# Other orders of the same work in a hybrid decoder block: z blocks ahead for one SSM unit, gate tiles loaded elsewhere, three FFN blocks side by side, last residual pairs by halves

## The chip, the core and the metric

The kernel runs on one core of a Trainium2 chip. The metric is the time of one execution in microseconds (us) of device time. Five engines work side by side, each in the order of its own queue: TensorE (PE: matrix products, with PEld for its weight loads), VectorE (DVE), ScalarE (ACT), GpSimd (POOL) and SyncE (SP, which here issues DMAs). A wait for another engine's result stops everything that stands behind it in the same queue.

## The reference

One decoder block over 256 positions of width 2048, in fp32. Two token mixers read the same normed input and are merged by sigmoid gates; a SwiGLU FFN follows.

```python
h = modulate(rms_norm(x, w), shift, scale)          # adaLN from c
ssm_z, ssm_xbc, ssm_dt, gdn_qkv, gdn_z, gdn_beta, gdn_a, gate_ssm, gate_gdn = split(h @ w_in)
y_ssm = mamba2_ssd_mixer(ssm_z, ssm_xbc, ...) @ w_ssm_proj     # conv, chunked scan, norm, 8 groups
y_gdn = gated_deltanet_mixer(gdn_qkv, gdn_z, ...) @ w_gdn_proj # conv, triangular solve, scan, 32 heads
m = sigmoid(gate_ssm) * y_ssm + sigmoid(gate_gdn) * y_gdn
x = x + gate * (m @ w_o)
x = x + gate2 * ffn(modulate(rms_norm(x), ...))     # silu(a) * b, then w_dn
out = rms_norm(x, w)
```

## The kernel before, in words

All weights come in blocks of 128 x 1024 fp32 (512 KB). For every block `load_next` issues the DMA into `raw` on SP's queue, lets ACT copy it to `hi` (L146) and DVE take `lo = raw - hi` (L148), so that a product is made of three: hi*hi, hi*lo and lo*hi. A block is one item of a queue. It costs TensorE 24 matmuls of 128 x 256 (L221 to L223, `lin_items`; L245 to L247, `quad_items`) or, for the z blocks, 12 of 128 x 512 (L268 to L270, `z_items`).

`pump()` is the clock of the program text. Each call loads blocks until four are ready, issues the matmuls of the oldest one, takes at most a few of the waiting posts (what follows a finished bank: convolution, gate, residual) and then one step of the running mixer, which is a Python generator: a `yield n` lets about n*R blocks pass before the next step. R is `RG[hu]` for the Gated DeltaNet (GDN) units `gdn_mix`, hu = 0 to 7, and `R_S` for the SSM units `ssm_mix`, g = 0 to 7. A block with `need` or `late_need` may be issued only when so many mixers are done; while it stands first in the queue, only mixer steps are issued, with no matmuls of weights between them.

While a unit is mixed, the blocks of the next unit are the cover: `g_in` and `s_in` append twelve to sixteen blocks for q, k, v or x, B, C and eight z blocks, and `proj_items` appends eight blocks that multiply the unit before by its output matrix (w_gp or w_sp) and add it to `accg` (L592). In the first SSM unit the eight w_gp blocks also gate the sum: `gate_g_post` (L984) reads a tile `ggt` that `gg_load` (L977) fetches from DRAM into one of two buffers.

The mixer steps that matter below, by the names of their tiles: at the head of a GDN unit `squares` and `ssq` (sums of squares of q and k), `N`/`T` and `seg` (decay exponents: `seg_rhs` makes the inputs on ACT, `seg_exp` two matmuls and an exp), `kq`; later `Tm` and `tv`; at its end `var`, `o` and `ot` (norm and transposition of the output, with a reciprocal root of 12 small POOL operations between). In an SSM unit `xt`, `cb`, `rh`/`rl` and `seg`, `yb`, `yo`, `yt`.

After the last unit come the merge, w_o, the second norm (`rf`, then 16 tiles `h2h`/`h2l`), w_gu, w_dn and the final norm. `res_post` adds a finished bank to the residual `accs` in two halves (L1204) and squares it (L1206); `ps_sq` sums the squares over partitions. At the FFN's entry `quad_items` cuts K into four quarters: an item of w_gu needs four h2 tiles only, and pairs of banks take their first quarters one after the other.

Of the kernel before, what the change touches and what calls it, by code (L numbers as in the profile page):

```python
# [19 lines left out]
P = 128  # L20
# [16 lines left out]

RG = [1.0] * 7 + [0.95]
R_M = 1.2
Q3 = [0, 8, 1, 9, 2, 10, 3, 11, 4, 12, 5, 13, 6, 14, 7, 15]  # L40
Y_SUB = [7] + [9] * 7
R_S = 1.6
# [32 lines left out]
def block_kernel(ctx: ExitStack, tc: tile.TileContext, xT, cvec, vec, dskip, consts,  # L75
# [132 lines left out]

    def lin_items(blocks, xh, xl, nk, done, need=0, sync=False, late_need=0):
        hold = {}  # L210
# [14 lines left out]
        for bi, src in enumerate(blocks):  # L225
            last = bi == len(blocks) - 1
            post = [lambda f=f: f(hold["ps"]) for f in done] if last else []
            add_item(src, mk(bi), post, late_need if last and late_need else need, sync and bi == 0)

    def quad_items(src, n, xh, xl, done, sync=False):  # L230
        bank_of = {}

        def mk(q, j):
            def mm(hi, lo):
                ah, al = xh(), xl()
                if q == 0:
                    bank_of[j] = plin.tile([P, 2, S], F32, tag="lin", name="ps_lin") if j < 3 else \
                        bank("ps_lin", (P, 2, S))
                ps = bank_of[j]
                for t in range(2):  # L240
                    for k in range(4):
                        kt = 4 * q + k
# [11 lines left out]

    def z_items(blocks, unit, extra=None):
        pss = {}
# [23 lines left out]
        for b in range(8):  # L280
            ex = extra[len(extra) * b // 8:len(extra) * (b + 1) // 8] if extra else []
            add_item(blocks[b], mk(b), ([lambda: done(0), lambda: done(1)] if b == 7 else []) + ex)

# [335 lines left out]

    def s_in(g, need=0, extra=None):  # L620
        unit = {}
        for pr in range(3):
            i = 6 * g + 2 * pr
            lin_items([w_s[g, 4 * pr + b] for b in range(4)], hh, hl, KT,
                      conv_posts(lambda ps: ps, VC_S + 4 * i, VCB_S + i, in_tile(unit, pr, 6)),
                      late_need=need if pr == 0 else 0)
        z_items(w_sz[g], unit, extra)
        return unit
# [87 lines left out]
    def gdn_mix(hu, units):  # L716
        unit = units[hu]
        nxt = units[hu + 1] if hu + 1 < NHU else None
        if hu == 0:
# [4 lines left out]
            seg_in, seg_out, squares, ssq, kq, scales, n_tile, store = gdn_head(hu, unit)  # L724
            squares()
            seg_in(0)
            yield 1
            ssq()
            seg_out(0)
            yield 1  # L730
            seg_in(1)
            kq()
            yield 1
            seg_out(1)
# [73 lines left out]
        for c in range(2):  # L808
            V.tensor_tensor(Tm[c].rearrange("p h (b j) -> p h b j", j=16),
                            Tp[:, 4 * c:4 * c + 4, :].unsqueeze(2).broadcast_to([P, 4, 8, 16]),  # L810
                            mid(bmask.rearrange("p (b j) -> p b j", j=16), 4), MUL)
        yield 1 if hu == 0 else 2
        for c in range(2):
# [175 lines left out]
    def ssm_mix(g, unit):  # L989
# [115 lines left out]
    for g in range(NG):  # L1105
        gens.append((ssm_mix(g, unit[NHU + g]), mark + DS, R_S if g < 7 else 1.0))
        if g + 1 < NG:
            gg = [lambda: None] * 6 + [lambda: gg_load(0), lambda: None]
            unit.append(s_in(g + 1, G0 + NHU + g, gg if g == 0 else None))
        else:  # L1110
# [88 lines left out]
    def res_post(j, gate, pool):  # L1199
        def f(ps):  # L1200
            x2 = pools["accs"]
            for t in range(2):
                i = 2 * j + t
                V.scalar_tensor_tensor(x2[:, i, :], ps[:, t, :], gate[:, i:i + 1], x2[:, i, :], MUL, ADD)  # L1204
            sq = pool.tile([P, 2, S], F32, tag="th" if j else "cacc", name="sq", bufs=1 if j or pool is not gl_ else NCA)
            A.activation(sq, x2[:, 2 * j:2 * j + 2, :], AF.Square)  # L1206
            if j == 0:
                sqa["a"] = sq
            elif j < 7:
                G.tensor_tensor(sqa["a"], sqa["a"], sq, ADD)  # L1210
            else:
                sqa["b"] = sq
        return [f]

    quad_items(w_o, 3, lambda: pools["m"][0], lambda: pools["m"][1], lambda j: res_post(j, ada[:, 32:48], gl_), sync=True)
    for j in range(3, 8):
        lin_items([w_o[j, b] for b in range(4)], lambda: pools["m"][0], lambda: pools["m"][1], KT,
                  res_post(j, ada[:, 32:48], gl_))
    n_wo = st_["added"]
# [32 lines left out]
    with tc.tile_pool(name="ff", bufs=1) as ff:  # L1252
# [7 lines left out]
        for t in range(KT + 1):  # L1260
            if t in (5, 9, 13):
                for _ in range(6):
# [12 lines left out]
        for j in range(8):  # L1275
            lin_items([w_dn[j, b] for b in range(11)], fh, fl, FT, res_post(j, gf, ff))
        ada_fin(80, 96)
# [116 lines left out]
```

## Time and profile before

| what | value |
|---|---|
| timed executions | median 2765.83 us (2764.89 to 2770.86, 3 runs) |
| profiled execution | 2744.2 us |
| its span, first to last instruction | 2742.4 us |
| mean granted TensorE clock | 0.988 |
| busy in the span | TensorE 97%, DVE 69%, ACT 50%, POOL 11% |

The profiled execution is 21.6 us shorter than the timed median; what is worked out from the trace is a difference and is carried over to the median as it stands.

### The profile page before, as it was taken

How to read it: one execution, taken by the hardware profiler on the slowest of the kernel's cores; microseconds unless marked ns; L12 is line 12 of the kernel's file. 1: busy time of each engine (PE TensorE's matmuls, PEld its weight loads, DVE VectorE, ACT ScalarE, POOL GpSimd, SP SyncE). 2: the span in 40 equal slices, each digit the busy share in tenths (PEclk: the TensorE clock that was granted, in tenths of full speed). 3: DMA queues.
4: the chain of work that ended last, by engine and by line, in shares of the span. 5: the costliest groups of instructions: out<-in, count | busy, mean ns of one | idle time of the engine just before them, and what ended most of it. 6: DMA issues, size and time to landing. Idle time of an engine off the chain costs nothing.

```text
span 2742.4 us, 51781 instructions
## 1 busy us (share of the span) xinstructions
PE 2665.7 (97%) x20930; PEld 2547.5 (93%) x20930; DVE 1884.0 (69%) x2794; ACT 1371.5 (50%) x2250; POOL 306.7 (11%) x684
## 2 busy tenths in 40 slices
PE   6999999999999999989999999999999999999998
PEld 5889899999999999988899989999989999999997
DVE  7787767769687786857767667768666666655444
ACT  3325554655546455544666656554444444444442
POOL 0000312303123131210000000002100000000000
PEclk8999999999999999999999999999999999999999
DMA  8886657566575665735545445447756666655553
GB/s 334 299 325 231 208 173 253 182 208 229 168 248 175 227 213 173 253 131 179 190 156 177 167 163 176 162 153 268 241 178 216 228 224 225 228 199 194 192 193 131
DMA packets 183283, 566.90 MB, mean 207 GB/s; under 512 B 34753, under 2 KB 43777, under 8 KB 183041
## 3 DMA queue, kind: packets, MB, share of 16 engines
q1 hardware_dynamic: 154306, 552.56, 59.0%
q10 hardware_dynamic: 28736, 11.01, 1.5%
q8 instruction: 164, 2.69, 0.4%
q14 instruction: 77, 0.63, 0.1%
HBM read 552.49 MB, written 11.01 MB: 205 GB/s over the span
## 4 chain that ended last, share of the span: by engine, by line
PE 64%; issue 21%; DVE 6%; DMA 4%; POOL 3%; ACT 2%; SPq 0%; ACTq 0%; DVEq 0%; POOLq 0%
PE ps_lin L221 14%; PE ps_lin L223 14%; PE ps_lin L222 14%; PE ps_z L268 2%; PE ps_z L270 2%; PE ps_z L269 2%; DMA araw<-in_w_ada 2%; DVE lo L148 2%; PE ps_lin L246 1%; PE tw L831 1%; PE td L839 1%; PE ps_q L406 1%; PE ps_lin L245 1%; PE ps_lin L247 1%; ACT hi L146 1%
## 5 line engine op out<-in xcount | busy, mean ns | idle before, releaser
L148 DVE TENSOR_TENSOR lo<-raw,hi 128x1024 fp32r<-128x1024 f32 x825 | 1012.3, 1232 | 673.4 <-ACT hi L146 670.6
L146 ACT CAST hi<-raw 128x1024 fp32r<-128x1024 f32 x825 | 860.5, 1049 | 527.1 <-PE ps_lin L222 259.5
L221 PE MATMUL ps_lin<-hh,hi 128*128 128x256 f32 x1792 | 510.1, 285 | 0.0
L222 PE MATMUL ps_lin<-hl,hi 128*128 128x256 f32 x1792 | 501.8, 280 | 0.0
L223 PE MATMUL ps_lin<-hh,lo 128*128 128x256 f32 x1792 | 501.7, 280 | 0.0
L222 PEld LDWEIGHTS ps_lin<-hl,hi 128*128 128x128 f32 x1792 | 340.3, 190 | 3.7 <-issue 2.4
L221 PEld LDWEIGHTS ps_lin<-hh,hi 128*128 128x128 f32 x1792 | 339.7, 190 | 4.1 <-issue 2.4
L223 PEld LDWEIGHTS ps_lin<-hh,lo 128*128 128x128 f32 x1792 | 340.7, 190 | 0.0
L223 PE MATMUL ps_lin<-h2h,lo 128*128 128x256 f32 x1216 | 335.7, 276 | 0.0
L222 PE MATMUL ps_lin<-h2l,hi 128*128 128x256 f32 x1216 | 335.6, 276 | 0.0
L221 PE MATMUL ps_lin<-h2h,hi 128*128 128x256 f32 x1216 | 335.6, 276 | 0.0
L221 PE MATMUL ps_lin<-yh,hi 128*128 128x256 f32 x896 | 255.0, 285 | 3.1 <-DVE accg L592 3.1
L222 PE MATMUL ps_lin<-yl,hi 128*128 128x256 f32 x896 | 250.0, 279 | 0.0
L223 PE MATMUL ps_lin<-yh,lo 128*128 128x256 f32 x896 | 249.9, 279 | 0.0
L223 PEld LDWEIGHTS ps_lin<-h2h,lo 128*128 128x128 f32 x1216 | 228.3, 188 | 0.2 <-DVE lo L148 0.2
L221 PEld LDWEIGHTS ps_lin<-h2h,hi 128*128 128x128 f32 x1216 | 228.3, 188 | 0.0
L222 PEld LDWEIGHTS ps_lin<-h2l,hi 128*128 128x128 f32 x1216 | 228.3, 188 | 0.0
L268 PE MATMUL ps_z<-hi,hh 128*128 128x512 f32 x512 | 206.8, 404 | 0.0
L270 PE MATMUL ps_z<-hi,hl 128*128 128x512 f32 x512 | 201.1, 393 | 0.0
L269 PE MATMUL ps_z<-lo,hh 128*128 128x512 f32 x512 | 200.6, 392 | 0.0
L223 PE MATMUL ps_lin<-fh,lo 128*128 128x256 f32 x704 | 194.3, 276 | 0.0
L221 PE MATMUL ps_lin<-fh,hi 128*128 128x256 f32 x704 | 194.3, 276 | 0.0
(328 smaller groups left out, 5416.6 us busy)
## 6 DMA issues: line engine op xcount, KB each, us to landing
raw<-in_w_gu SPq DMA_DIRECT2D x176, 512.0 KB, 4.2
raw<-in_w_g SPq DMA_DIRECT2D x143, 512.0 KB, 4.6
raw<-in_w_ada SPq DMA_DIRECT2D x128, 512.0 KB, 5.1
raw<-in_w_s SPq DMA_DIRECT2D x96, 512.0 KB, 4.1
raw<-in_w_dn SPq DMA_DIRECT2D x88, 512.0 KB, 4.3
araw<-in_w_ada SPq DMA_DIRECT2D x64, 512.0 KB, 7.8
raw<-in_w_gz SPq DMA_DIRECT2D x64, 512.0 KB, 4.5
raw<-in_w_gp SPq DMA_DIRECT2D x64, 512.0 KB, 3.9
```

The costliest lines, as they stand in the source:

```text
L146: A.copy(hi, raw)
L148: V.tensor_sub(lo, raw, hi.bitcast(F32))
L221: T_.matmul(ps[:, t, :], hi[:, s], h_, start=kt == 0, stop=False)
L222: T_.matmul(ps[:, t, :], hi[:, s], al[:, kt, :], start=False, stop=False)
L223: T_.matmul(ps[:, t, :], lo[:, s], h_, start=False, stop=kt == nk - 1)
L245: T_.matmul(ps[:, t, :], hi[:, s], h_, start=kt == 0 and t == 0, stop=False)
L246: T_.matmul(ps[:, t, :], hi[:, s], al[:, kt, :], start=False, stop=False)
L247: T_.matmul(ps[:, t, :], lo[:, s], h_, start=False, stop=kt == KT - 1 and t == 1)
L268: T_.matmul(pss[c], hh[:, kt, cs], hi[:, s], start=kt == 0, stop=False)
L269: T_.matmul(pss[c], hh[:, kt, cs], lo[:, s], start=False, stop=False)
L270: T_.matmul(pss[c], hl[:, kt, cs], hi[:, s], start=False, stop=kt == KT - 1)
L406: T_.matmul(ps[:, t, :], hi[:, s], x1[:, kt, :], start=first, stop=last)
```

## The change

It changes the order of work and where some of it is kept; the arithmetic and the weights moved stay as they are.

1. The head of GDN unit 0 issues `squares` and `ssq` one step later, behind the inputs of `seg` and its matmuls. The step ahead of `tv` waits two blocks for every unit (before: one for unit 0). `Y_SUB` of unit 1 goes from 9 to 8, by which unit 1's solve has one step fewer to wait.
2. `RG[7]` goes from 0.95 to 1.0.
3. For SSM unit 1 the z blocks stand ahead of the w_s blocks, and the last of them carries the `late_need`.
4. `gg_load` fetches into slices of `accs`, which is idle until SSM unit 1 is projected; the eight fetches are issued by posts of the w_s blocks of pairs 1 and 2, not by the gate's own posts.
5. In `ssm_mix` `seg_rhs` of the first half is issued ahead of the first `yield`, right behind the transposition.
6. The last pair of `res_post` (w_o and w_dn) is added and squared half by half, and with it the first half can be taken earlier (`half`).
7. At the FFN's entry three items are issued side by side: K tile by K tile, each of the three banks in turn.

```diff
-RG = [1.0] * 7 + [0.95]
+RG = [1.0] * 8
-Y_SUB = [7] + [9] * 7
+Y_SUB = [7, 8] + [9] * 6
...
     def lin_items(blocks, xh, xl, nk, done, need=0, sync=False, late_need=0, half=None):
...
             post = [lambda f=f: f(hold["ps"]) for f in done] if last else []
+            if half and (bi + 1) * BLK > nk >= bi * BLK:
+                post = [lambda: half(hold["ps"])]
...
+    def s_in(g, need=0):
         unit = {}
+        if g == 1:
+            z_items(w_sz[g], unit, None, need)
         for pr in range(3):
...
+            if g == 1 and pr:
+                for b in range(4):
+                    src, mm, post, *rest = items[b - 4]
+                    items[b - 4] = (src, mm, [lambda q=4 * pr - 4 + b: gg_load(q)] + post, *rest)
+        if g != 1:
+            z_items(w_sz[g], unit)
...
-            squares()
             seg_in(0)
             yield 1
-            ssq()
+            squares()
             seg_out(0)
             yield 1
+            ssq()
             seg_in(1)
+            yield 1
             kq()
-            yield 1
...
-        yield 1 if hu == 0 else 2
+        yield 2
...
-        gg_of[pr] = gl_.tile([P, 2, S], F32, tag="cacc", name="ggt", bufs=NCA)
+
+        gg_of[pr] = pools["accs"][:, 2 * pr:2 * pr + 2, :]
         nc.sync.dma_start(gg_of[pr], ggd[:, pr])
...
-            if pr + 1 < 8:
-                gg_load(pr + 1)
...
+        rhs = seg_rhs(sp_, triu, 0, 8 * g)
         yield 1
...
-        rhs = seg_rhs(sp_, triu, 0, 8 * g)
         yield 1
...
+        def tail(t, ps):
+
+            x2 = pools["accs"]
+            i = 14 + t
+            if t == 0:
+                sqa["b"] = pool.tile([P, 2, S], F32, tag="th", name="sq", bufs=1)
+            V.scalar_tensor_tensor(x2[:, i, :], ps[:, t, :], gate[:, i:i + 1], x2[:, i, :], MUL, ADD)
+            A.activation(sqa["b"][:, t, :], x2[:, i, :], AF.Square)
...
+            if t == 5:
+
+                while len(ready) < LA + 1:
+                    load_next()
+                side_by = [ready.popleft() for _ in range(3)]
+                for k in range(4):
+                    for mm, _, _, _, hi, lo in side_by:
+                        mm(hi, lo, (k,))
+                st_["mm"] += 3
+                for _ in range(3):
+                    pump()
```

TensorE at the end of GDN unit 7, before: the last three matmuls of a block, the two transpositions `ot` and the next block.

```order
L221 MATMUL ps_lin<-hh,hi 128x256
L222 MATMUL ps_lin<-hl,hi 128x256
L223 MATMUL ps_lin<-hh,lo 128x256
L946 MATMUL ot<-cst,o_13652 128x128 x4
L946 MATMUL ot<-cst,o_13653 128x128 x4
L221 MATMUL ps_lin<-hh,hi 128x256
L222 MATMUL ps_lin<-hl,hi 128x256
```

After, around the first `ot`, where z blocks (12 matmuls of 128 x 512 each) now stand:

```order
L270 MATMUL ps_z<-hi,hh 128x512
L271 MATMUL ps_z<-lo,hh 128x512
L272 MATMUL ps_z<-hi,hl 128x512
L956 MATMUL ot<-cst,o_13649 128x128 x4
L270 MATMUL ps_z<-hi,hh 128x512
L271 MATMUL ps_z<-lo,hh 128x512
```

The two `ot` stood next to each other; now the second one stands 24 matmuls, or two z blocks, behind the first.

SP's queue in SSM unit 0, before: each fetch of a gate tile but the first waits there for a buffer, with weights behind it.

```order
L144 DMA raw<-in_w_sz 128x1024
L144 DMA raw<-in_w_gp 128x1024 x3
L977 DMA ggt<-ggd 128x512
L144 DMA raw<-in_w_gp 128x1024 x2
L977 DMA ggt<-ggd 128x512
L144 DMA raw<-in_w_gp 128x1024
L977 DMA ggt<-ggd 128x512
L144 DMA raw<-in_w_gp 128x1024
L977 DMA ggt<-ggd 128x512
L144 DMA raw<-in_w_gp 128x1024
```

After, the eight fetches stand among the loads of the last w_s and the first w_gp blocks:

```order
L144 DMA raw<-in_w_s 128x1024 x5
L988 DMA accs<-ggd 128x512
L144 DMA raw<-in_w_s 128x1024
L988 DMA accs<-ggd 128x512 x3
L144 DMA raw<-in_w_s 128x1024
L144 DMA raw<-in_w_gp 128x1024
L334 DMA raw<-in_w_ada 128x1024
L144 DMA raw<-in_w_gp 128x1024
L988 DMA accs<-ggd 128x512
L144 DMA raw<-in_w_gp 128x1024
L988 DMA accs<-ggd 128x512 x3
L144 DMA raw<-in_w_gp 128x1024 x5
```

They go to tiles of their own, four of them ahead of the first w_gp block's load.

DVE at the end of w_dn, before, from the last but one output pair to the final norm:

```order
L148 TENSOR_TENSOR lo<-raw,hi 128x1024 x11
L1204 SCALAR_TENSOR_TENSOR accs<-ps_lin,gf,accs 128x256 x2
L148 TENSOR_TENSOR lo<-raw,hi 128x1024 x7
L1204 SCALAR_TENSOR_TENSOR accs<-ps_lin,gf,accs 128x256 x2
L321 RECIPROCAL rstd<-rstd 128x256
L1290 SCALAR_TENSOR_TENSOR accs<-accs,vs,rstd 128x256 x13
```

After:

```order
L148 TENSOR_TENSOR lo<-raw,hi 128x1024 x11
L1212 SCALAR_TENSOR_TENSOR accs<-ps_lin,gf,accs 128x256 x2
L148 TENSOR_TENSOR lo<-raw,hi 128x1024 x6
L1229 SCALAR_TENSOR_TENSOR accs<-ps_lin,gf,accs 128x256
L148 TENSOR_TENSOR lo<-raw,hi 128x1024
L1229 SCALAR_TENSOR_TENSOR accs<-ps_lin,gf,accs 128x256
L324 RECIPROCAL rstd<-rstd 128x256
L1320 SCALAR_TENSOR_TENSOR accs<-accs,vs,rstd 128x256 x13
```

The last pair's two additions stood together behind seven subtractions; now the first of them stands one subtraction earlier, and the second alone.

## Rows read from the trace of the kernel before

**Rows 1.** Page, part 1: busy time of TensorE, share of the span, instructions.

```profile
PE 2665.7 (97%) x20930; PEld 2547.5 (93%) x20930; DVE 1884.0 (69%) x2794; ACT 1371.5 (50%) x2250; POOL 306.7 (11%) x684
```

**Rows 2.** Waits of TensorE, whole span: us in total, times, longest.

```profile
PE ot L946 <- DVE o L922: 6.8, 2, 6.6
...
PE ssq L674 <- ACT sq L667: 3.2, 1, 3.2
PE ps_lin L221 <- DVE accg L592: 3.1, 3, 2.1
...
PE yt L1084 <- ACT yn L1077: 2.6, 2, 1.5
PE tv L816 <- DVE Tm L809: 2.5, 1, 2.5
PE seg L582 <- ACT rl L574: 1.9, 4, 0.7
...
PE seg L581 <- ACT rh L574: 1.0, 1, 1.0
```

**Rows 3.** Windows of half clock; busy of each engine, PEclk the granted clock.

```profile
281.50:288.33 6.83, 6.59 (x29) 6.40 (x30) 3.35 (x8) 5.89 (x15) 0.78 (x4) 0.50 0.06 19
339.53:342.94 3.41, 3.41 (x18) 3.41 (x18) 3.34 (x6) 2.17 (x4) 0.00 (x0) 0.50 0.86 282
1206.51:1213.34 6.83, 5.10 (x24) 4.95 (x25) 2.05 (x6) 0.69 (x1) 0.75 (x4) 0.50 0.23 83
1291.84:1295.26 3.42, 3.42 (x17) 3.42 (x17) 2.28 (x4) 2.09 (x5) 0.00 (x0) 0.50 0.48 152
1994.99:2001.82 6.83, 4.21 (x14) 3.38 (x15) 5.33 (x11) 3.30 (x6) 0.00 (x0) 0.50 0.01 2
```

**Rows 4.** Timeline of ACT at the first GDN unit's head: start, duration.

```profile
281.07 1.14 ACT L667 ACTIVATE sq<-qkv 128x512 f32<-128x512 f32 x2
282.11 1.26 ACT L574 ACTIVATE N<-sl_r,dAh 128x128 fp32r<-128x128 f32 x4
```

**Rows 5.** Timeline of TensorE at the same head.

```profile
281.74 3.57 PE L674 MATMUL ssq<-ones,sq 128*128 128x1 f32 x16 [3.22 <-ACT sq L667]
285.17 0.77 PE L581 MATMUL seg<-N,triu_r 128*128 128x512 f32 x1
```

**Rows 6.** Timeline of TensorE at the end of the last GDN unit.

```profile
1201.04 0.60 PE L946 MATMUL ot<-cst,o 128*128 128x128 f32 x4
1208.24 1.17 PE L946 MATMUL ot<-cst,o 128*128 128x128 f32 x4 [6.60 <-DVE o L922]
```

**Rows 7.** Timeline of DVE at the end of the last GDN unit.

```profile
1192.98 0.68 DVE L592 TENSOR_TENSOR accg<-ps_lin,accg 128x512 f32<-128x512 f32 x1
```

**Rows 8.** Waits of SP's DMA queue, 1265 to 1300 us.

```profile
SPq L977 <- DVE accg L984: 26.7, 6, 10.4
```

**Rows 9.** Windows, first SSM unit: steps and z blocks, then w_gp blocks.

```profile
1235.00:1267.70 32.70, 32.70 (x178) 27.63 (x177) 26.96 (x39) 18.66 (x35) 0.00 (x0) 1.00 0.62 210
1267.70:1296.10 28.40, 25.25 (x201) 24.63 (x200) 20.06 (x32) 12.28 (x20) 4.99 (x12) 0.94 0.40 137
```

**Rows 10.** DVE by line and shape, 1210 to 1300 us: count, busy, mean.

```profile
L148 DVE TENSOR_TENSOR lo<-raw,hi 128x1024 fp32r<-128x1024 f32 x24 | 29.0, 1222 | 19.8 <-ACT hi L146 19.7
...
L296 DVE SCALAR_TENSOR_TENSOR cacc<-ps_lin,vs,cacc 128x254 f32<-128x254 f32 x6 | 2.9, 482 | 0.2
...
L1043 DVE TENSOR_TENSOR M<-M,cbm 128x512 f32<-128x512 f32 x3 | 2.1, 684 | 0.0
```

**Rows 11.** Timeline of TensorE, the FFN's first block and the next one's start.

```profile
1997.61 0.58 PE L245 MATMUL ps_lin<-h2h,hi 128*128 128x256 f32 x1 [3.54 <-ACT h2h L1267]
...
2003.04 0.28 PE L245 MATMUL ps_lin<-h2h,hi 128*128 128x256 f32 x1
```

**Rows 12.** Timeline at the kernel's end.

```profile
2727.37 0.88 DVE L1204 SCALAR_TENSOR_TENSOR accs<-ps_lin,gf,accs 128x256 f32<-128x256 f32 x2 [8.69 <-PE ps_lin L223]
2728.34 0.63 ACT L1206 ACTIVATE sq<-accs 128x512 f32<-128x512 f32 x1 [10.91 <-DVE accs L1204]
```

More of the change, by code (lines that the diff above doesn't have):

```diff
@@ L207, in rsqrt, with lin_items @@
         return y
-    def lin_items(blocks, xh, xl, nk, done, need=0, sync=False, late_need=0):
+    def lin_items(blocks, xh, xl, nk, done, need=0, sync=False, late_need=0, half=None):
         hold = {}
@@ L233, in mk, with mm @@
         def mk(q, j):
-            def mm(hi, lo):
+            def mm(hi, lo, ks=range(4)):
                 ah, al = xh(), xl()
-                if q == 0:
+                if q == 0 and ks[0] == 0:
                     bank_of[j] = plin.tile([P, 2, S], F32, tag="lin", name="ps_lin") if j < 3 else \
@@ L240, in mm @@
                 for t in range(2):
-                    for k in range(4):
+                    for k in ks:
                         kt = 4 * q + k
@@ L253, in quad_items, with z_items @@
                          0, sync and q == 0 and j == 0)
-    def z_items(blocks, unit, extra=None):
+    def z_items(blocks, unit, extra=None, late_need=0):
         pss = {}
@@ L281, in z_items @@
             ex = extra[len(extra) * b // 8:len(extra) * (b + 1) // 8] if extra else []
-            add_item(blocks[b], mk(b), ([lambda: done(0), lambda: done(1)] if b == 7 else []) + ex)
+            add_item(blocks[b], mk(b), ([lambda: done(0), lambda: done(1)] if b == 7 else []) + ex,
+                     late_need if b == 7 else 0)
     def conv_posts(src_of, cw, cb, dst):
@@ L618, in in_tile @@
         return dst
-    def s_in(g, need=0, extra=None):
+    def s_in(g, need=0):
         unit = {}
+        if g == 1:
+            z_items(w_sz[g], unit, None, need)
         for pr in range(3):
@@ L626, in s_in @@
                       late_need=need if pr == 0 else 0)
-        z_items(w_sz[g], unit, extra)
+            if g == 1 and pr:
[4 more added lines that the diff above has]
+            z_items(w_sz[g], unit)
         return unit
@@ L1107, in block_kernel @@
         if g + 1 < NG:
-            gg = [lambda: None] * 6 + [lambda: gg_load(0), lambda: None]
-            unit.append(s_in(g + 1, G0 + NHU + g, gg if g == 0 else None))
+            unit.append(s_in(g + 1, G0 + NHU + g))
         else:
@@ L1201, in f @@
             x2 = pools["accs"]
-            for t in range(2):
+            for t in range(2 if j < 7 else 0):
                 i = 2 * j + t
                 V.scalar_tensor_tensor(x2[:, i, :], ps[:, t, :], gate[:, i:i + 1], x2[:, i, :], MUL, ADD)
+            if j == 7:
+                tail(1, ps)
+                return
             sq = pool.tile([P, 2, S], F32, tag="th" if j else "cacc", name="sq", bufs=1 if j or pool is not gl_ else NCA)
@@ L1208, in f @@
                 sqa["a"] = sq
-            elif j < 7:
+            else:
                 G.tensor_tensor(sqa["a"], sqa["a"], sq, ADD)
[L1211 to L1215, printed above, removed]
+        def tail(t, ps):
[5 more added lines that the diff above has]
+            A.activation(sqa["b"][:, t, :], x2[:, i, :], AF.Square)
+        return [f], (lambda ps: tail(0, ps)) if j == 7 else None
+    quad_items(w_o, 3, lambda: pools["m"][0], lambda: pools["m"][1], lambda j: res_post(j, ada[:, 32:48], gl_)[0], sync=True)
     for j in range(3, 8):
-        lin_items([w_o[j, b] for b in range(4)], lambda: pools["m"][0], lambda: pools["m"][1], KT,
-                  res_post(j, ada[:, 32:48], gl_))
+        done, half = res_post(j, ada[:, 32:48], gl_)
+        lin_items([w_o[j, b] for b in range(4)], lambda: pools["m"][0], lambda: pools["m"][1], KT, done, half=half)
     n_wo = st_["added"]
@@ L1260, in block_kernel @@
         for t in range(KT + 1):
-            if t in (5, 9, 13):
+            if t == 5:
[8 more added lines that the diff above has]
+                    pump()
+            if t in (9, 13):
                 for _ in range(6):
@@ L1275, in block_kernel @@
         for j in range(8):
-            lin_items([w_dn[j, b] for b in range(11)], fh, fl, FT, res_post(j, gf, ff))
+            done, half = res_post(j, gf, ff)
+            lin_items([w_dn[j, b] for b in range(11)], fh, fl, FT, done, half=half)
         ada_fin(80, 96)
```

## The prediction

> **What bounds the kernel now.** I read the page first. TensorE is busy 97% of the span [rows 1], so only what TensorE loses can be won: the stretches in which it waits, and those in which it works at half clock. The list of TensorE's waits gives the first. Those that the change touches are few: 6.8 us for `o` in two waits, of which one is 6.6; 3.2 for `sq`; 3.1 for `accg` in three waits, the largest 2.1; 2.5 for `Tm`; 1.9 in four and 1.0 in one for the inputs of `seg` [rows 2]. The windows give the second: after the waits for `sq`, `Tm`, `o` and `accg`, and after the last w_o pair, the granted clock is 0.50, that is 1.2 instead of 2.4 GHz, for 6.83, 3.41, 6.83, 3.42 and 6.83 us [rows 3]. Work done there costs twice its time, so half of the busy time in such a window is the price: 5.10 of PE in the third costs 2.55. A wait of 1.5 us (`yt`, [rows 2]) has no such window behind it; one of 2.1 has.
>
> The Trainium skill, "TensorE: Matmul & The Clock Gate", section "Terms", prices throttled time by its whole length times the share of pulses left out. By that the windows behind `Tm`, `o` and `accg` would cost 6.83 us together. The rows say 5.97, because in the third window PE idled 1.7 us, which is already counted as a wait; I take the rows.
>
> **Part by part.** Sums are of the profiled execution, 2744.2 us.
>
> *Head of GDN unit 0.* Now TensorE idles 3.22 us for the squares, then runs `ssq` for 3.43 us at half clock (281.74 to 285.17), then `seg` [rows 5]. ACT squares at 281.07 and makes the first `N` at 282.11, the second 1.16 later [rows 4]. After the change ACT makes N in the place of the squares, so `seg` can start at about 281.07 + 1.26 = 282.3 and ends when the second set and 0.6 us have passed, about 284.1: the next block starts 2.1 us earlier than at 286.2. Against that `ssq` comes later at full clock, half of 3.43 = 1.7 us, and 2.1 us more of blocks run in the half-clock window, 1.1 us. Sum +0.7. Below: the window moves with the shorter idling, -2.1. Above: `ssq` falls into half clock too, or a second wait arises for the squares, +2. The norms that hang on `ssq` come a block later; between `scales` and its reader stand blocks, and no wait of TensorE stands there now.
>
> *`tv`.* One more block (2.73 us: 24 matmuls at 0.114) between `Tm` and `tv` covers the 2.5 us wait and takes the window behind it: -2.5 and half of 3.41 = -1.7, together -4.2. Bound from below of the gain: the clock falls anyway, -2.5. `Y_SUB` takes unit 1's delay back, so that the later units stand as before.
>
> *End of GDN unit 7.* The two `ot` stood together; the second waited 6.60 us, until 1208.24 [rows 6]. The chain behind it is POOL's reciprocal root and `o` on DVE. With the z blocks ahead, eight instead of four blocks lie before the one that must wait for the unit, and two z blocks of 2.75 us stand between the two `ot`. From the first (1201.04 + 0.60) to the second are 6.6 us, less 5.5, so 1.1 us would be left if the chain stands as now against the first `ot`; 0 if the first z block comes later than the chain. I take 0.4. The clock is held: -2.55. A new wait: the second bank of the z items is that of the last-but-one w_gp block, which DVE adds at 1192.98 for 0.68 [rows 7]. The first z block would start at 1191.6 and reach its fourth matmul at 1192.3, so it waits 1.4 us. Sum -6.6 - 2.55 + 0.4 + 1.4, about -7.4; bounds -9.2 and -5.0 (that 2.55 of clock is lost again to the new waits).
>
> *`seg_rhs` earlier.* rh and rl are made one step sooner, so that the `seg` waits of 1.9 + 1.0 us [rows 2] shrink. Only the first half of each unit moves; the second's inputs hang on the same ACT queue. I take half, -1.5; bounds 0 and -2.9.
>
> *Gate tiles.* SP waits 26.7 us in six waits for buffers that DVE's gating frees [rows 8], with weights queued behind each. TensorE sees 3.1 us of that as waits for `accg`, and 1.7 of half clock. In tiles of their own, the fetches wait for nothing of the gate: -4.8. Each of the eight fetches is 256 KB on the same queue, half a weight block each, while weights now have four blocks of lead; I put no price on them. What comes new: the w_s blocks with their convolutions now share the time of the SSM unit's own steps, where z blocks stood. That is DVE's burden (first rival); +0.5 for it, and +1.0 where convolution posts stand ahead of ACT's `rh` and the next casts. Sum -3.3; bounds -4.8 and +1.
>
> *w_o's end and the FFN's entry.* TensorE waits 3.5 us for the first h2 tile and needs 5.43 us for the first block, 1997.61 to 2003.04 [rows 11], where 2.73 is the full pace. But the clock is at 0.50 until 2001.82 [rows 3], and at half clock a block takes 5.46: the tiles are hardly what it waits for. Three blocks side by side use a tile three times, which is worth the short waits between tiles (about 0.6). The halves of the last pair save some 0.7 of 0.88 + 0.63 (the same two operations as in [rows 12]). Sum -1.3; bounds 0 and -4 (the clock rises a window earlier, 3.41 x 0.5, too).
>
> *Kernel's end.* After the last matmul stand an addition of two halves, 0.88, and a square, 0.63 [rows 12]. With the first half taken earlier, half of each goes, and a start: -1.0. The first half lies in the bank that TensorE is writing the second half to, so the first matmul of the next block but one must wait for DVE's reading, 0.65. Sum -0.35; bounds -1.0 and +0.3. The Trainium skill, "PSUM — Partial Sum Buffer", section "PSUM bank collisions raise a hardware error", has the two engines kept apart per bank, not per address: by it the wait stands, and by addresses alone the sum would be -1.0. No row of before shows such a half read.
>
> Altogether +0.7 - 4.2 - 7.4 - 1.5 - 3.3 - 1.3 - 0.35 = -17.35 us: the profiled execution at 2726.9, the median at 2765.8 - 17.4 = **2748 us**. All bounds at once would give -28 and -4.
>
> **Rivals.** *First, DVE becomes the bound in SSM unit 0.* The twelve w_s blocks with the unit's steps are about 38.8 us for TensorE; for DVE 12 subtractions of 1.22, 18 convolution steps of 0.48, 3 products of 0.69 and some 11 us of the unit's own operations (groups of the same view, `M` with 2.1 the largest [rows 10]), 36.5 us. The eight w_gp blocks are 22.6 against about 23. Together 59.5 of 61.4 us. The two windows of now show DVE at 82% and, with the gate's waits in it, 71% [rows 9]. Held to 82% DVE would need 72.6 us, 11 more than TensorE: 2759. For it speaks the order of each post behind a cast; against it that DVE idles there because casts wait for late weights. If posts only spread, it is the +0.5 of the sum.
>
> *Second, the waits move.* The waits at `Tm`, `o` and `sq` go, but the new ones (the z bank, the second `ot`, `seg` for N) grow to the size of the 2.1 us for `accg`, which has a half-clock window behind it: each then brings about 2 us of wait and 2 of half clock. With all three the sum loses some 9 us: 2757. For it: the 1.4 is not far from that; against it: the 1.5 for `yt` has none.
>
> *Third, more comes back than the sum has:* unit 0's window goes, all `seg` waits go, the FFN's entry gains a window: -2.1 instead of +0.7, -2.9, -4, which makes -24: 2741.
>
> *Fourth, slower.* The one mechanism that could do it is DVE in SSM unit 0: the loss there would have to pass 17.4 + 5.5 = 23 us, so 59.5 us of its work in 84 us, below 71% busy, what the window with the gate's waits shows today [rows 9]. That would need weights as late as now; time then about 2772.
>
> *Fifth, no change:* the pieces give half and DVE takes the rest, 2761 to 2771.
>
> **How the numbers follow.** Chances: the forecast (2743 to 2755) 0.52, DVE bound in the unit 0.13, waits move 0.13, more comes back 0.12, no change 0.07, slower 0.03. A measurement of this kernel tells about 0.2%, 5.5 us, from no change. Below 2760.3 lie the first four, but a third of the first rival's chance lies above; so faster 0.86, same 0.11, slower 0.03. For 8 in 10 I take 2736 to 2760: it holds the forecast, most of both middle rivals and most of the third, with 3 us of spread of the runs.
>
> **What would show it.** No wait of `tv` for `Tm`, and no half clock at 340. `ot` waits under 1.5 us in place of 6.6, and the six waits of SP for `accg` gone. `seg` of unit 0 waits some 4 us for N. TensorE's waits at the first w_gp blocks of SSM unit 0 near zero. Wrong would be: waits of PE for `lo` or `hi` there of over 10 us in all, or idle stretches of over 2 us in the z blocks.

## The result and the profile after

| | before | changed |
|---|---|---|
| timed executions beside each other | 2765.36 us median (2748.32 to 2770.86, 4) | 2727.47 us median (2723.64 to 2731.89, 4) |
| profiled execution | 2744.2 | 2726.35 |
| its span | 2742.4 | 2724.6 |

The ratio of the times is 0.9875, with a 95% interval from 0.9829 to 0.9922. The median was forecast at 2748, range 2736 to 2760: the medians differ by 38 us, not by 17 (the means by 35). The profiled execution, on the other hand, was forecast at 2726.9 and is 2726.35. So the sum over the trace came out, in part by luck, as will be seen, and the step from the trace to the median did not. The experiments are mostly about that step.

The waits of TensorE in the changed kernel, over the whole span (us in total, times, longest; the parts that the change touches):

```profile
PE seg L584 <- ACT N L577: 3.9, 1, 3.9
...
PE ps_lin L247 <- ACT h2h L1296: 3.5, 1, 3.5
...
PE ps_lin L221 <- DVE accg L595: 2.4, 1, 2.4
PE tw L841 <- ACT Vm L827: 2.0, 3, 1.2
...
PE ps_z L270 <- DVE var L921: 1.3, 1, 1.3
...
PE ps_lin L221 <- DVE accs L1229: 0.7, 1, 0.7
PE seg L585 <- ACT rl L577: 0.5, 3, 0.2
...
PE ot L956 <- DVE o L932: 0.2, 1, 0.2
```

Against [rows 2]: the waits for `o` (6.8) and `Tm` (2.5) are gone but for 0.2, `seg` waits 3.9 for N in place of `ssq`'s 3.2 for the squares, and the new waits stand where they were looked for, 1.3 at the second z bank and 0.7 at the bank of which DVE reads a half. SP waits for the gating no more, where [rows 8] had 26.7. TensorE's waits for `accg`, 2.4 where they were 3.1, look as if they had stayed, but it is another wait. Before, TensorE waited for the additions of the third to the fifth w_gp block, while SP waited for the ring; now it waits once, for that of the first, where the prediction looked for nearly nothing. Before, in TensorE's timeline:

```profile
1291.67 0.40 PE L221 MATMUL ps_lin<-yh,hi 128*128 128x256 f32 x1 [2.12 <-DVE accg L592]
```

After, in the timelines of ACT, DVE and TensorE:

```profile
1261.23 0.63 ACT L1070 ACTIVATE jk<-xN 128x512 f32<-128x512 f32 x1 [3.38 <-DVE xN L1068]
...
1261.86 0.62 ACT L306 ACTIVATE cth<-cacc 128x512 f32<-128x512 f32 x1
...
1262.51 0.69 DVE L307 SCALAR_TENSOR_TENSOR qkv<-cth,cacc 128x512 f32<-128x512 f32 x1 [1.37 <-ACT cth L306]
...
1264.58 0.68 DVE L595 TENSOR_TENSOR accg<-ps_lin,accg 128x512 f32<-128x512 f32 x1
...
1265.41 0.36 PE L221 MATMUL ps_lin<-yh,hi 128*128 128x256 f32 x1 [2.39 <-DVE accg L595]
```

The addition for which TensorE waits stands on DVE behind the last convolution's product. DVE idles 1.37 us for that product's input `cth`, and ACT makes `cth` only behind `jk`, the sum of squares of the SSM unit's own norm, for which it has waited 3.38 us for DVE. `tw` waits for `Vm` a little more.

The half-clock windows of the changed kernel between the first 50 us and the tail (engines' busy times, then the granted clock):

```profile
279.81:286.64 6.83, 5.90 (x24) 5.30 (x25) 3.93 (x7) 5.48 (x12) 0.00 (x0) 0.50 0.22 74
1266.26:1269.67 3.41, 3.41 (x18) 3.41 (x17) 3.34 (x7) 0.00 (x0) 1.17 (x2) 0.50 0.73 246
1983.06:1986.47 3.41, 3.41 (x17) 3.41 (x18) 2.46 (x6) 2.26 (x4) 0.00 (x0) 0.50 0.02 5
```

The windows behind `Tm` and `o` are gone, the one at the FFN's entry is half as long, and one stands behind the new wait for `accg`. The trace of before has one more window at the FFN's entry, which [rows 3] leaves out and the changed kernel's trace does not have:

```profile
2039.36:2042.78 3.42, 3.42 (x19) 3.42 (x18) 1.23 (x1) 1.59 (x2) 0.00 (x0) 0.50 0.15 53
```

To place the gain, the same matmuls are timed in both traces, between the same numbers in TensorE's order. In the windows view each stretch below has about 1000 or 2000 of them (x behind PE busy). Before: the head of unit 0 to `tv`; the end of GDN unit 7 and SSM unit 0; the end of w_o and the FFN's entry:

```profile
251.40:399.50 148.10, 142.41 (x1002) 132.57 (x1001) 103.12 (x173) 84.01 (x160) 33.30 (x77) 0.97 0.57 191
1171.95:1460.62 288.67, 276.50 (x2002) 257.89 (x2001) 196.41 (x295) 165.87 (x314) 21.84 (x60) 0.98 0.49 166
1982.20:2112.70 130.50, 123.11 (x1003) 118.79 (x1003) 86.27 (x121) 58.41 (x80) 1.30 (x1) 0.96 0.58 196
```

The changed kernel, the same three:

```profile
249.30:394.40 145.10, 140.58 (x1002) 130.55 (x1002) 101.69 (x167) 82.56 (x158) 30.17 (x74) 0.98 0.59 195
1165.89:1444.32 278.43, 273.01 (x2002) 254.16 (x2001) 197.07 (x295) 165.35 (x310) 23.53 (x60) 0.99 0.52 175
1967.30:2094.60 127.30, 120.26 (x1003) 116.73 (x1002) 84.87 (x119) 58.68 (x81) 1.29 (x1) 0.99 0.59 197
```

That is -3.0, -10.2 and -3.2 us, 16.4 of the 17.8 between the two spans. The rest is 2.1 us before 250 us, where the change moves nothing, and differences both ways, the largest in w_o just ahead of the third stretch: the same 600 matmuls without a wait took 68.0 us in the trace of before and 70.7 in the other.

### The profile page after: what moved, and what is told of

Same layout as the page of the kernel before. It is cut to its first block, busy times and chain, and to the rows that moved or that the text cites. A ratio compares the mean times of both kernels' runs of the same rounds, so it can differ in the third digit from the quotient of the medians.

```text
span 2724.6 us, 51782 instructions
## 1 busy us (share of the span) xinstructions
PE 2658.1 (98%) x20930; PEld 2540.3 (93%) x20930; DVE 1882.3 (69%) x2794; ACT 1371.5 (50%) x2252; POOL 316.6 (12%) x684
## 4 chain that ended last, share of the span: by engine, by line
PE 62%; issue 21%; DVE 7%; POOL 4%; DMA 3%; ACT 2%; SPq 0%; ACTq 0%; DVEq 0%; POOLq 0%
PE ps_lin L221 14%; PE ps_lin L223 14%; PE ps_lin L222 14%; PE ps_z L270 2%; PE ps_z L272 2%; PE ps_z L271 2%; DVE lo L148 2%; DMA araw<-in_w_ada 2%; DVE araw L337 1%; PE tw L841 1%; POOL tm L797 1%; PE td L849 1%; PE ps_lin L248 1%; POOL Gt L799 1%; PE ps_lin L249 1%
## 5 line engine op out<-in xcount | busy, mean ns | idle before, releaser
L222 PE MATMUL ps_lin<-fl,hi 128*128 128x256 f32 x704 | 194.5, 276 | 0.0
```

The costliest lines, as they stand in the source:

```text
L222: T_.matmul(ps[:, t, :], hi[:, s], al[:, kt, :], start=False, stop=False)
```

## The experiments

Executions in a set ran on one chip, with the kernel before among them; sets ran on different chips. A first set timed both kernels again and took the change apart.

The kernel before, unchanged (`before_again`).

> The kernel before, unchanged, for more executions and a second trace. The two traces at hand differ by 17.8 us, the timed medians by 38. Theory one (the profiled execution of before was a short one, and what is longer in most others lies in waits that the change removes, those for the gate tiles above all): times spread from 2744 to 2771, and this trace shows more idle time of TensorE between 1230 and 1300 us than the 3.1 us of the first. Rival (the early, DMA-bound part or the chip makes the spread, and the change has no part in it): the extra time lies ahead of 270 us or is spread evenly, and kernels timed on this chip differ by about 18 us.

Twelve executions: five at 2739.6 to 2755.2 us, seven at 2770.0 to 2776.4, none between. The 35 of the kernel before that ran beside them: 23 at 2740 to 2755, 12 at 2769 to 2779. This trace is of a long one, 2773.7. Both theories look in the wrong place: up to the FFN it runs at most 5 us behind the first trace. What differs is one steady stretch of the FFN, here in the windows view of the first trace (TensorE only: length, busy, matmuls; clock; DMA):

```profile
2200.00:2600.00 400.00, 400.00 (x3531) 1.00 0.63 211
```

and of the long execution:

```profile
2200.00:2600.00 400.00, 400.00 (x3398) 1.00 0.60 204
```

TensorE is 100% busy at full clock in both, and waits for nothing. Yet one makes 3531 matmuls in 400 us, 113.3 ns each, the other 3398, 117.7 ns each. From 2062 us to the end of w_dn there are some 5,900 of them: 5,900 x 4.4 ns = 26 us, which is the distance of the two groups of executions. So the same kernel has **two paces**, and keeps one from the last wait at the FFN's entry to the end. Of the 20 traces taken in all, four are at the slow pace there (here, in `gg_ring`, `z_gg_only` and `after_seg`), all four of long executions. Of the other 16 one is of an execution as long, `rest_late_seg_v`, which lost its time elsewhere. The mean duration of a row tells it too, 276 against 281 ns in the grouped view of this window, but nothing in the lists of waits does. Among the mixers both paces occur in every trace and change at groups of small matmuls.

The changed kernel again (`after_again`).

> The changed kernel, unchanged, on the same chip as the others of this set. Theory one: some 30 to 35 us under the kernel before (ratio 0.988). Rival: 18 us under it (ratio 0.9935).

2730.56 median: nine at 2724.3 to 2738.5, three at 2754.8 to 2760.4; ratio 0.9927 (0.9884 to 0.9970). Among executions of the short kind, the medians are 2746.3 before and 2729.3 changed: 17.0 us.

The changed kernel with the ring of two gate buffers (`gg_ring`), z blocks first as in the change (the first fetch is then issued by the post of the last w_s block; that hunk is left out):

```diff
...
-        gg_of[pr] = pools["accs"][:, 2 * pr:2 * pr + 2, :]
+        gg_of[pr] = gl_.tile([P, 2, S], F32, tag="cacc", name="ggt", bufs=NCA)
...
+            if pr + 1 < 8:
+                gg_load(pr + 1)
```

> The changed kernel, but the gate tiles in the ring of two buffers again, each fetch issued by the gate ahead of it; z blocks stay first. By the prediction this gives back 3 to 5 us. Theory one: it gives back 15 us or more, and the spread of the executions with it. Rival: 3 to 5 us, spread as in the changed kernel.

2745.2 median, seven of twelve at 2734 to 2745 (median 2740.3), five at 2765 and above. Short ones against short ones that is 11 us given back, where the prediction had 3 to 5; its spread is as wide as that of the kernel before. The traces have it in the second stretch above: 290.3 us here, 278.3 to 278.8 in five traces of the changed kernel.

The kernel before with z blocks first, gate tiles in `accs` and RG[7] = 1.0 only (`z_gg_only`): points 2 to 4 of the change, with their hunks as shown there.

> The kernel before with the z blocks of SSM unit 1 first, the gate tiles in accs and RG[7] at 1.0, nothing else. By the prediction -7.4 - 3.3, about -11 us. Theory one: -25 or more. Rival: about -11.

2760.65 median, and no number can be read from that: eleven of twelve were at 2757.7 to 2771.6, one at 2742.3, and the trace is at the slow pace. A kernel's median says as much of its share of long executions as of its work.

**What sets the pace.** In the traces the pace changes only at a break in the stream. If a break sets it, a few idle matmuls behind the last wait of the FFN's entry should set it anew. Two kinds were tried, on the changed kernel and on the kernel before (the result is read by nobody):

```diff
+    def break_pace(hi):                       # after_seg, before_seg
+        b = bank("seg", (P, 2, S))
+        T_.matmul(b, hi[:, 0:P], F_["h"][:, 0:2, :], start=True, stop=False)
+        T_.matmul(b, hi[:, 0:P], F_["l"][:, 0:2, :], start=False, stop=True)
...
+    def break_pace(hi):                       # all kernels whose name ends in _v
+        b = bank("v0")
+        for h in range(4):
+            for i in range(2):
+                T_.matmul(b[:, h, :], pools["accs"][:, 2 * h + i, 0:P], pools["accs"][:, 2 * h + i, P:S],
+                          start=i == 0, stop=i == 1)
```

> The changed kernel with two idle matmuls of 128x512 ahead of the seventh w_gu group's first block (their result is read by nobody). In the traces so far every pair like it (the GDN units' seg) is followed by matmuls at 113.3 ns start to start, never at 117.8. Theory (TensorE keeps one of two paces from the last wait at the FFN's entry to the end, 5800 matmuls, and that is what makes the executions of one kernel differ by 26 us): all executions lie within 2722 to 2740, none near 2757, and the trace shows 113.3 throughout. Rival (the pace is set by something outside the order on TensorE, such as memory or the other engines): about a quarter stay at 2755 to 2760 as before, and the pair costs its 0.5 us.

> The changed kernel with eight idle fp32 matmuls of 128x128 at the same place (nobody reads them); in the traces the like group v of the GDN units is always followed by 117.8 ns. Theory: all or most executions at 2750 to 2762, and the trace shows 117.8 ns through w_gu and w_dn. Rival: three in four executions stay at 2724 to 2740.

> The kernel before with the two idle 128x512 matmuls at the same place. Theory: all executions at 2738 to 2755, none at 2765 to 2778; the changed kernel with the same pair is then 16 to 19 us shorter, the difference that the first two traces showed. Rival: half of the executions stay at 2765 to 2778.

The pair does not set it, against the theory: three of twelve stay long in `after_seg` (2757.1 to 2764.1), two in `before_seg` (2769.2, 2771.8). In the trace of `after_seg`, a long one, the pace is the same ahead of the pair and behind it:

```profile
2046.20:2061.00 14.80, 14.80 (x128) 1.00 0.54 179
2062.40:2077.20 14.80, 14.80 (x128) 1.00 0.59 188
```

The eight small ones did set it, the other way than I had read from the GDN units: all twelve of `after_v` lie at 2728.9 to 2744.6. Its trace comes to the place at the slow pace and leaves it at the fast one, 128 and 133 matmuls in 14.8 us:

```profile
2046.90:2061.70 14.80, 14.80 (x128) 1.00 0.55 179
2064.50:2079.30 14.80, 14.80 (x133) 1.00 0.60 192
```

`after_v2`, the same kernel on another chip, shows the same; the other eight traces with these matmuls come to the place at the fast pace already. All ten leave it at the fast one, and the ten timings (117 executions) have no second group 26 us up. So an edit of TensorE's stream alone is enough to keep the slow pace away. That memory or another engine has a part where there are no such matmuls is not excluded.

The changed kernel without the three blocks side by side (`no_sbs`), and the kernel before with them alone (`sbs_only`):

```diff
-            if t == 5:
-                side_by = [ready.popleft() for _ in range(3)]
...
-            if t in (9, 13):
+            if t in (5, 9, 13):
```

> The changed kernel with the FFN's entry as before (six blocks one after the other, no three side by side), no idle matmuls. By the prediction 0.6 us are lost. If the entry's order decides how often the fast pace is met, half or more of the executions are at 2755 to 2762 and the median is there or between; if it is chance of a few ns whatever the order, the share stays near the changed kernel's 3 of 12.

> The kernel before with only the FFN's entry of the change: three blocks side by side. No idle matmuls. Theory (the entry's order by itself makes the fast pace frequent, as 10 of 12 executions were slow without it and 3 of 12 with it): at most 3 of 12 executions at 2765 to 2778, the others at 2738 to 2752. Rival (the share hangs on the instant at which the entry is met, and any edit ahead of it draws anew): 4 or more of 12 slow.

Without them ten of twelve were long (median 2758.56). This looked as if the side-by-side entry made the fast pace frequent. But on the kernel before the same entry made nine of twelve long (median 2778.08). So the order of the program at the entry does not decide it alone, and the shares differ from kernel to kernel: what they hang on is not shown.

The two entries are not the same in time, though, which also bears on what point 7 is worth. In `sbs_only` TensorE waits longer for `h2l` than in the kernel before, and its long executions are longer than those of the kernel before beside it (medians 2779.1 and 2771.6). These are the waits of `sbs_only` and of `before_v` (below) from 1985 to 2110 us:

```profile
PE ps_lin L246 <- DVE h2l L1280: 5.7, 9, 1.4
```

```profile
PE ps_lin L248 <- DVE h2l L1279: 2.6, 9, 0.3
```

What stands in the way is a piece of the adaLN product (`ada_half`, on DVE); the program issues one after every so many calls of `pump()`. The three blocks side by side make three calls fewer, and the piece falls right ahead of the h2 tiles, three times; so it does in `rest_v` (below), whose DVE has, at the first of the three places:

```profile
2011.64 1.23 DVE L148 TENSOR_TENSOR lo<-raw,hi 128x1024 fp32r<-128x1024 f32 x1 [1.49 <-ACT hi L146]
2012.78 1.22 DVE L339 SCALAR_TENSOR_TENSOR raw<-raw,cact 128x1024 f32<-128x1024 f32 x1
2013.93 0.08 DVE L339 DVE_READ_ACCUMULATOR raw<-raw,cact 128x1 f32 x1
2013.93 0.47 DVE L1300 SCALAR_TENSOR_TENSOR htmp<-accs,wsf,rf 128x256 f32<-128x256 f32 x1
2014.32 0.48 DVE L1303 SCALAR_TENSOR_TENSOR h2l<-htmp,ada,h2h 128x256 fp32r<-128x256 f32 x1
```

The three kernels with the side-by-side entry but not z first (`sbs_only`, `rest_v`, `rest_late_seg_v`) have 5.7 to 6.0 us of these waits, the 17 other traces 2.4 to 3.1. No run moves that piece alone.

**The work itself, at one pace.** With the eight idle matmuls kernels can be compared to a few us.

> The kernel before with the eight idle fp32 matmuls of 128x128 ahead of the seventh w_gu group; behind them all twelve executions of the changed kernel kept the fast pace. Theory (the prediction's sum is right for executions of one pace, and the rest of the timed difference is how often each kernel falls into the slow one): all or nearly all at 2744 to 2758, median about 17 us above the changed kernel with the same matmuls, so 2751. Rival (the change also makes the fast executions shorter than the traces say, or the kernel before slow for another reason): the median stays 25 us or more above, or executions at 2765 to 2778 stay frequent.

> The kernel before with the eight idle matmuls, on the chip of gg_only_v: 2742 to 2755, median 2748.

> The changed kernel with the eight idle matmuls once more, now on one chip with the next kernel: 2731 to 2736, all executions at the fast pace.

Medians: before 2748.7 (2742.2 to 2754.3) and on another chip 2745.0 (2740.7 to 2749.2); changed 2733.5 and 2735.7 (2729.1 to 2740.3). At one pace the change is worth 9 to 15 us, whichever pair is taken, none of them on one chip. The short executions of the unmodified kernel before, which ran in every set, allow for the chip: against their medians `before_v` and `before_v2` lie 3.4 and 0.6 above, `after_v` and `after_v2` 10.4 and 11.7 below, so 11 to 15. The forecast's 17 lies just above that, and is what the short executions of one chip gave; the rival's 25 is out.

`z_gg_v` and `gg_ring_v` are `z_gg_only` and `gg_ring` with the idle matmuls. `gg_only_v` is, against `z_gg_v`:

```diff
-RG = [1.0] * 8
+RG = [1.0] * 7 + [0.95]
...
-        if g == 1:
-            z_items(w_sz[g], unit, None, need)
...
-        if g != 1:
-            z_items(w_sz[g], unit)
+        z_items(w_sz[g], unit)
```

> The kernel before with only the z blocks of SSM unit 1 first, the gate tiles in accs and RG[7] at 1.0, and the same eight idle matmuls. By the prediction's terms -7.4 and -3.3: 10 to 11 us under the kernel before with these matmuls. Rival (these parts do less, the rest of the change more): under 7 us.

> The changed kernel with the gate tiles in the ring of two buffers, and the eight idle matmuls. By the prediction 3 to 5 us are given back against the changed kernel with these matmuls. Rival from the first timing of the ring (fast executions of 2738 against 2729): 8 to 10 us, since the waits for the ring now meet w_s blocks with their convolutions.

> The kernel before with only the gate tiles in accs, fetched by the posts of the w_s blocks; z blocks and RG[7] as before; with the eight idle matmuls. By the prediction's terms -3.3 (and the second ot's 6.6 us wait with its half clock stays): 3 to 5 us under the kernel before on this chip. Theory from the traces so far (the two hang together: each alone moves the wait, both together take it away): 3 us or less. Rival (the gate tiles are the whole gain): 10 to 14 us.

On the chip of the first `before_v` (2748.7): z blocks, gate tiles and RG[7] alone 2734.2 (2731.5 to 2737.8), -14.5 where the terms gave 10 to 11; the whole change but with the ring 2742.5, that is 8.3 above, and 8 to 9 above the whole change when each is held against its own chip, so the rival's 8 to 10 rather than the prediction's 3 to 5. On the chip of `before_v2` (2745.0): the gate tiles alone 2739.0, -6.0, a little more than the prediction's 3 to 5 and between what the two theories expected. Each part by itself leaves a wait. In `gg_only_v` TensorE waits, from 1160 to 1335 us, no more for `accg`, but still for `o`:

```profile
PE ot L953 <- DVE o L929: 6.6, 1, 6.6
PE seg L585 <- ACT rl L577: 1.3, 2, 0.7
PE seg L584 <- ACT rh L577: 1.1, 1, 1.1
```

With z blocks first and the ring (`gg_ring_v`) `o` is no longer waited for, and `accg` more than before:

```profile
PE ps_lin L223 <- DVE accg L597: 7.1, 5, 3.6
...
PE ps_z L272 <- DVE var L923: 1.3, 1, 1.3
```

The 3.6 are for the addition of the first w_gp block, as the 2.4 of the changed kernel are; the other waits are for later ones, while SP waits for the ring.

The same 2000 matmuls as in the second stretch above took 288.5 us in `before_v`, 283.1 with the gate tiles alone, 290.9 with z first and the ring, and with both in `z_gg_v`:

```profile
1170.84:1451.53 280.69, 273.72 (x2002) 254.78 (x2001) 196.50 (x293) 165.43 (x310) 23.50 (x60) 0.99 0.54 172
```

`rest_v` is the changed kernel with points 2 to 4 undone; `rest_late_seg_v` and `z_gg_tv_v` are, against `rest_v` and against `z_gg_v`:

```diff
-        rhs = seg_rhs(sp_, triu, 0, 8 * g)
         yield 1
...
+        rhs = seg_rhs(sp_, triu, 0, 8 * g)
         yield 1
```

```diff
-Y_SUB = [7] + [9] * 7
+Y_SUB = [7, 8] + [9] * 6
...
-        yield 1 if hu == 0 else 2
+        yield 2
```

> The changed kernel without the z blocks first, the gate tiles in accs and RG[7] at 1.0 (these as before), with the eight idle matmuls: what is left are the head of unit 0, the step ahead of tv, seg_rhs, the halves and the FFN's entry. By the prediction +0.7 - 4.2 - 1.5 - 1.3 - 0.35, about 6.7 us under the kernel before with these matmuls. Rival: they bring nearly nothing apart from the wait at tv (3 us or less).

> The rest of the change (as in rest_v, with the eight idle matmuls), but seg_rhs of the SSM units again behind the products of cb, where it stood before. Theory (made earlier, rh and rl stand ahead of the casts and of BN on ACT, and the ring of gate tiles then meets a later queue): 5 us or more under rest_v, at 2745 to 2749. Rival (seg_rhs does not matter; the loss is elsewhere): within 2 us of rest_v, 2752 to 2756.

> The kernel before with the z blocks of SSM unit 1 first, the gate tiles in accs, RG[7] at 1.0, the two-block step ahead of tv with Y_SUB of unit 1 at 8, and the eight idle matmuls; no other part of the change. By the terms measured so far (-14.5 for the first three, about -4 for tv): 2730, so 3 us under the whole change with these matmuls. Rival: the parts left out bring the 2 to 3 us of the sum, and it is 2 us above.

The rest of the change, without these parts, does not gain the 6.7 us forecast but loses: 2754.15 (2745.0 to 2758.5) against 2748.7 on one chip. Putting `seg_rhs` back does not mend it: 2756.1, on another chip. The trace of `rest_v` is its shortest execution, 2745.0; it is 2.7 us shorter than `before_v`'s in the first of the three stretches, near the forecast 3.5, then needs 292.2 us for the second stretch, where `accg` is waited for longer, and 2.2 us more than `before_v` at the FFN's entry, with the piece of adaLN ahead of the tiles:

```profile
PE ot L951 <- DVE o L927: 6.6, 1, 6.6
PE ps_lin L223 <- DVE accg L597: 5.8, 3, 3.1
```

The step ahead of `tv` brings nothing on top of the two large parts either: 2730 was expected, and `z_gg_tv_v` has 2736.9 beside `after_v2` 2735.7, and `z_gg_v` on its chip 2734.2. Held against the short executions of its own chip, `z_gg_v` lies 11.1 below: the whole change is not shown to be worth more than its z blocks, gate tiles and RG[7]. The trace of `z_gg_tv_v` is of its longest execution, 2748.3, and shows a wait one step on, at `tw`, in units 1 and 3 (390 to 720 us), each with a half-clock window behind it:

```profile
PE tw L841 <- ACT Vm L827: 4.4, 2, 2.3
```

## Why the prediction was right and wrong

**The step that failed** is the one at the end of its reckoning, "the median at 2765.8 - 17.4", and the sentence ahead of the prediction that a difference in the trace is carried over to the median as it stands. The table showed the profiled execution 21.6 us under the median, outside the three timed ones, and I passed over it. It meant that the kernel before has executions of two kinds, and that the trace was of a short one while the three timed ones were long. In all sets together 77 of 176 executions of the kernel before were long, three of 16 of the changed one. In the first comparison it was three of four against none of four. The median of before, 2765.36, lies among the long ones, 17.0 above the one short execution, 2748.32; that one lies 20.9 above the changed median, and the two make the 38. The first part is a matter of which kind was met, and the edits' work has no part in it; the second is near the forecast. On the larger set the ratio is 0.9927, -20 us. The range fell with the same step: it left 3 us for the spread of the runs, and took 5.5 us for telling a change, where the executions of the kernel before lie from 2740.0 to 2778.6 on one chip.

That the sum, -17.35, came within 0.5 us of the 17.8 between the two spans is in part luck: 2.1 us of it lie before 250 us, w_o was 2.7 us slower in the changed kernel's trace, and terms were off both ways. The kernel before and the changed kernel have five traces each, with and without idle matmuls. In us, between the same numbers in TensorE's order:

| matmuls | stretch | before, 5 traces | changed, 5 traces | `rest_v`, `rest_late_seg_v` |
|---|---|---|---|---|
| 1500 to 2500 | head of unit 0 to `tv` | 146.6 to 148.1 | 144.7 to 146.1 | 145.2, 144.8 |
| 2500 to 8500 | units 1 to 7 | 771.1 to 772.5 | 771.5 to 778.1 | 771.9, 781.8 |
| 8500 to 10500 | end of unit 7, SSM unit 0 | 288.5 to 290.6 | 278.3 to 278.8 | 292.2, 295.4 |
| 14500 to 15500 | w_o's end, FFN's entry | 129.2 to 131.4 | 127.3 to 130.8 | 131.4, 136.2 |

The terms, against these traces:

- Head of unit 0 and `tv`: forecast +0.7 and -4.2, measured -3.0 together in the first two traces, 0.5 to 3.4 in the ten; `seg` waits 3.9 + 0.4 for N, and no window stands at 340. The rival "the waits move" came true further on, with its clock price. Eleven traces are of kernels with the new step ahead of `tv`; in three of them (`after_seg`, `z_gg_tv_v`, `rest_late_seg_v`) units 1 to 7 take 778.1 to 781.8 us, with waits at `tw` of 1.1 to 2.3 us in units 1 and 3 and half clock behind them. All nine traces without the step have 771.1 to 772.5. The prediction had nothing for it.
- End of GDN unit 7 and gate tiles: -7.4 and -3.3 forecast, -10.2 in the stretch, which has a share of `seg_rhs` in it. The z bank's wait was forecast as 1.4 and is 1.3, with no half clock behind it; the second `ot` 0.4 and 0.2. But the split was wrong. The gate tiles alone brought 5.4 (288.5 to 283.1), more than the bound of 4.8, and took every wait for `accg` away; z first with RG[7] on top of them brought 2.4 more (to 280.7), not 7.4. Its order makes the new wait for the first w_gp block's addition, 2.4 us, in the first trace with 3.41 of half clock behind it (`after_again` has the wait and not the window). The nearest thing in the prediction is 1.0 for convolution posts that stand ahead of other work, under the gate tiles. That DVE has too much to do there, the first rival, is not what the trace shows, since DVE idles 1.37 us on the way to it. And z first while the ring stands brings nothing in this stretch: 290.3 and 290.9. Timed, `gg_ring_v` is 11.6 us shorter than `rest_v` on the same chip all the same, from which it differs by z first and RG[7] alone; 2 us of that stand at the FFN's entry in the two traces (129.4 and 131.4), and the rest is not explained. (The term's upper bound, with the 2.55 lost again, is -4.8, not -5.0.)
- `seg_rhs`: the waits for rh and rl fell from 2.9 to 0.5, against -1.5 forecast. The stretch is 1.9 to 2.4 us shorter than in `z_gg_only`, `z_gg_v` and `z_gg_tv_v` (280.7), where it is not moved.
- FFN's entry and w_o's end: -1.3 forecast, -3.2 in the first two traces; over five traces each the two kernels overlap. The second window of before, at 2039, is not in `before_again`, `before_seg` or `before_v`. The first became 3.41 us, the lower bound that I had named, in three traces of the changed kernel, and is 6.83 in `after_v` and `after_v2`. Whether three blocks side by side save anything is not shown; where the piece of adaLN falls ahead of the tiles they lose.
- Kernel's end: from matmul 15500 on +0.3; the bank's wait is 0.7 where 0.65 was forecast. The Trainium skill, "PSUM — Partial Sum Buffer", section "PSUM bank collisions raise a hardware error", has PSUM guarded by bank and quadrant, not by address. This case's trace agrees: the next matmul into the bank of which DVE reads the other half waits 0.7 us for that reading.

So the rest of the change loses in three places that the traces show: at `tw` in some executions, at the FFN's entry when z does not stand first, and in the stretch of SSM unit 0. How the 5 us of the timed medians divide among them is open, and so is why `accg` is waited for longer in `rest_v` than in the kernel before. Open stays above all why a given kernel draws a large or a small share of long executions. No version beat the changed kernel's short executions (2729); with the eight idle matmuls its spread falls from 2724 to 2760 to 2729 to 2745, at a median some 3 us higher, on another chip.

## What to carry to other kernels

Before a difference of traces is put on a median, hold the profiled execution's own time against all timed ones: a trace outside their range is a sign of two kinds of executions, and a sum that is right for one kind says nothing of their shares. In a stretch where an engine is always busy, count its instructions per us; a pace that differs by 4% shows in no list of waits. Two reorderings that both shorten one stretch are to be measured alone and together: here the second, forecast at 7.4 us, brought 2.4 on top of the first, since it made a wait of its own. And a wait of the same name and size after a change need not be the same wait: look where it stands.

## What the runs showed of the hardware

A long stream of 128x256 matmuls, three per pair of weight tiles, with a weight load each, runs on TensorE at one of two lasting paces at the same full clock: 113.3 or 117.7 ns from start to start (3531 or 3398 in 400 us). The pace held for 5,800 matmuls, and changed at short breaks in the stream. A pair of 128x512 matmuls left it as it was in the two traces with one; the eight fp32 matmuls of 128x128 were followed by the fast one in all ten traces with them, in two of them after the slow one. Why is not shown.
